# One more weight unit behind the ring's first round, and the norm rows made in expert 3

## The chip, the cores and the metric

The kernel runs on one core of a Trainium2 chip. The core has five engines that run their own instruction lists and wait for each other by semaphores: TensorE (PE, with its weight loads as PEld), VectorE (DVE), ScalarE (ACT), GpSimd (POOL) and SyncE (SP), which here does little but issue transfers. Transfers between HBM and the on-chip memory are carried by 16 DMA engines; SP and ACT each issue into a queue of their own. Time is device time of one execution in microseconds.

## What is computed

One layer of an encoder over 512 tokens of width 1024: three token mixers side by side (neighbourhood attention, grouped-query attention with rotary positions, cross-attention into 256 memory tokens), gated and merged, an output product w_out, a layer norm; then a mixture of 16 experts in which each expert picks its 64 best tokens, and a second layer norm.

```python
branches = jnp.stack([y_na, y_gqa, y_mem], axis=2)
proj = jnp.einsum('bsgk,gkd->bsgd', branches, w_branch[l])
merged = jnp.sum(gates * proj, axis=2)
x = layer_norm(DN_ALPHA * x + merged @ w_out, ln1_g[l], ln1_b[l])
# experts
aff = jax.nn.softmax(x @ w_router, axis=-1)
gate, idx = lax.top_k(jnp.swapaxes(aff, 1, 2), cap)      # 64 tokens each
h = jnp.einsum('becd,edf->becf', x[bidx, idx], w_gate_up)
hg, hu = jnp.split(h, 2, axis=-1)
ye = jnp.einsum('becf,efd->becd', jax.nn.silu(hg) * hu, w_down) * gate[..., None]
x = layer_norm(DN_ALPHA * x + scatter_add(ye, idx), ln2_g[l], ln2_b[l])
```

The experts' weights are float32, 16 x 12 MB, and each is read once.

## The kernel before

The program has no scheduler: every engine carries out its instructions in the order in which the Python code emits them, and a tile framework adds the waits. Tiles with the same tag share memory in turn.

**First half** (mixers, to L1189). PE multiplies weight units of 128 x 1024 that SP streams in (`Stream`, L142 to L192); ACT and DVE split each into a high and a low part (`hi_lo`, L96). Attention runs as a pipeline beside it: `run` (L787) takes one step of attention at the yields of the product generators, and one entry of the background list `bg`, if there is one. For each of the three column groups of grouped-query attention `rope_stages` (L372) gives such entries: s1 square, s2 root mean square, s3 scaling, s4 the rotation in six POOL operations (L402 to L405), then one or two of `sk`/`sq_` (L414, L423), which transpose the result on PE (`heads_T`, L411) and evict it by ACT and DVE. The entries of the last two groups, `a` and `b`, are put in order at L464; among them is `norm_hi`.

**Norm rows.** The gains and shifts of both layer norms are 15 rows of 1024 floats (`lnp`). They are loaded early on SP's queue (`load_norms`, behind the 14th weight unit), cast to a high part on ACT (`norm_hi`, L860) and completed by two DVE operations (`norm_mask`, `norm_lo`), all as background entries, into `gb`, which holds its memory to the end. `ln_row` (L1366) spreads one row over 128 partitions with a PE product; its first user is `residual` in expert 4.

**Second half** (experts, L1568 on). The weights come in units of 128 x 2048 floats (1 MB): `("gu", e, k)`, eight gate/up units of an expert, and `("dn", e, k)`, four down units. `_blocks` (L45) lists the 192 units in the order of their use and deals them, round by round, to the twelve buffers of `RING` (L32), ten of which hold two units. In the first round a block fills its buffer with one load of two units; in the second round (to the 36th unit) and among the last ten each unit is a load of its own. `Ring.load` (L806) issues a block's load on SP's queue; `Ring.upto` fills the first round when the buffers' earlier tenants are done (L977, L1111, L1190); later loads are issued by `Ring.done` (L831) when PE has used the units that the buffer held. SP carries out its loads in order, and with eight completion semaphores in turn it waits for the load eight issues earlier.

Expert e (loop at L1574): the first four (`lead`) gate/up units, with `h_transpose(e - 1)` ahead of the fourth; `down(e - 1)`; for odd e `slots_T(e // 2)`, which turns the one-hot slots of a pair of experts into `GTe` or `GT` (two "homes", used in turn); the other four gate/up units; `act_h(e)`, tanh on ACT and two products on DVE in tiles of the tag "t". After e = 3, 7 and 11 `gather` fetches the next four experts' tokens: 64 products on PE, in chunks of eight through the three "mm" banks, evicted alternately by DVE (L1263) and ACT (L1261). `combine` and `residual` run as side work between units.

The routing's arrays lie in one tile of the tag "bf" (`rt`, L904), among them the affinities `aff` (slot 0).

Of the kernel before, what the change touches and what calls it, by code (L numbers as in the profile page):

```python
# [9 lines left out]
F32 = mybir.dt.float32  # L10
F32R = mybir.dt.float32r
# [3 lines left out]
ALU = mybir.AluOpType  # L15
# [3 lines left out]
P = 128  # L19
D = 1024  # L20
S = 512
KD = 8
NT = 4
NEXP = 16
# [7 lines left out]
RING = (("Q2", 2), ("Q1", 2), ("Q5", 2), ("Q7", 2), ("Q4", 2), ("Q3", 2), ("Q6", 2), ("raw", 1), ("Q9", 2), ("VS", 1),  # L32
        ("G1", 2), ("M", 2))
# [7 lines left out]
def lead(e):  # L41
    return 2 if e == NEXP - 2 else 4


def _blocks():  # L45
    order = []
    for e in range(NEXP - 1):
        order += [("gu", e, k) for k in range(lead(e))]
        if e:
            order += [("dn", e - 1, k) for k in range(4)]  # L50
        order += [("gu", e, k) for k in range(lead(e), KD)]
    order += [("gu", NEXP - 1, k) for k in range(KD)]
    order += [("dn", e, k) for e in (NEXP - 2, NEXP - 1) for k in range(4)]
    blocks, i, r = [], 0, 0
    while i < len(order):
        for tag, n in RING:
            left = ROUNDS.get(tag, len(order)) - r
            if left > 0 and i < len(order):
                keys = order[i:i + n]
                i += n  # L60
                if r and (i < FULL or i > len(order) - N_SINGLE):
                    blocks += [(tag, h, [key]) for h, key in enumerate(keys)]
                else:
                    blocks.append((tag, 0, keys))
        r += 1
    return blocks
# [3 lines left out]
def layer_kernel(ctx: ExitStack, tc: tile.TileContext, xt, xn, first0, wu, bgate, rpb, gains, wrt,  # L70
                 lnp, lnt, wx, csn, nmask, tri, iota, out, dbg=None):
    nc = tc.nc
# [12 lines left out]
    def R(tag, shape, name, dt=F32, bufs=None):  # L85
        return rp.tile(shape, dt, name=name, tag=tag, bufs=bufs)
# [110 lines left out]
    after = {}  # L197
# [61 lines left out]
    nc.sync.dma_start(wr_t, wrt)  # L259
    lnT = cp.tile([P, 5, KD], F32, name="lnT")  # L260
    nc.sync.dma_start(lnT[:, :2], lnt)
    gb = cp.tile([15, D], F32R, name="gb")
    gb_s, gb_c, gb_t = (cp.tile([15, n], F32, name="gb_" + k)[:, :1] for k, n in (("s", 1), ("c", 1), ("t", 33)))
    ident_r = cp.tile([P, P], F32R, name="ident_r")
    gsel = cp.tile([15, 3], F32R, name="gsel")
# [173 lines left out]
    def g_gqa():  # L439
        kk = R("Q6", [P, 4, S], "kk", F32R)  # L440
        qs = R("Q4", [P, 8, S], "qs", F32R)
        ST["b01"] = b01 = R("Q5", [P, 4, 1024], "ropevg")
        b1t = b01[:, 2:4]
        vg = b1t[:, 0, :512].rearrange("p (m f) -> p m f", m=NT)
        ST.update(khh=kk[:, 0:2], klo=kk[:, 2:4], vg=vg, qs=(qs[:, 0:4], qs[:, 4:8]),
                  rope=(vs_t[:, 0], b1t[:, 1]), zr=b01[:, 0:2])
        rope = []
        for q in range(3):
            us = ws.take(2)
            zs = ST["A5" if q % 2 else "A6"][:, 1, :512 if q == 0 else 1024].rearrange("p (m c) -> p m c", m=NT)  # L450
# [12 lines left out]
        a, b = rope[1:]  # L463
        bg.extend([lambda: None, a[4], b[0], a[5], b[1], b[2], b[3], norm_hi, b[4], b[5]])  # L464

    def g_na_v():
        v = ST["b01"][:, 0:2].rearrange("p a (b f) -> p (a b) f", f=S)
# [330 lines left out]
    class Ring:  # L798
# [7 lines left out]
        def load(self):  # L806
            tag, h, keys = self.blocks[self.n]
            n = len(keys)
            src = wx[self.row:self.row + P * n].rearrange("(p j) (h c) -> p (j h) c", j=n, h=2)
            if tag not in self.home:  # L810
                self.home[tag] = R(tag, [P, 2 * dict(RING)[tag], D], f"w{self.n}")
            full = self.home[tag][:, 2 * h:2 * (h + n)]
            nc.sync.dma_start(full, src)
# [38 lines left out]
    norm_raw = []  # L852

    def load_norms():
        norm_raw.append(vs_t[:15, 1])
        nc.sync.dma_start(norm_raw[0], lnp)

    after[14] = [load_norms]

    def norm_hi():  # L860
        nc.scalar.copy(gb, norm_raw[0])

    def norm_mask():
        norm_raw.append(vs_t[:15, 0])
        nc.vector.tensor_scalar(norm_raw[1], gb.bitcast(F32), gb_c, None, op0=ALU.mult)

    def norm_lo():
        nc.vector.scalar_tensor_tensor(gb, norm_raw[0], gb_s, norm_raw[1], op0=ALU.mult, op1=ALU.add)


    run(g_mem())
    dump("mkT", ST["mkT"])
# [6 lines left out]
    yg = R("Q2", [P, 8, S], "yg", F32R)  # L879
    ST["y1"] = (yg[:, 0:4], yg[:, 4:8])  # L880
    at.add([GqaUnit(hp, m) for hp in range(4) for m in range(NT)])
    bg.extend([norm_mask, norm_lo])
    run(g_branch(2, True), 1.0, 3)
    run(g_na_v(), 1.0)
    at.drain()
# [16 lines left out]
    run(g_branch(1, False, between), 0.5)  # L902

    rt = R("bf", [P, 12, 64], "rt")  # L904
    aff = rt[:, 0].rearrange("p (m e) -> p m e", m=NT)
    cnt = rt[:, 2:4].rearrange("p a (m e) -> p m a e", m=NT)
    st_all = rt[:, 5:7].rearrange("p a b -> p (a b)")[:, :96].rearrange("p (m q s) -> p m q s", m=NT, q=4)
    ones_f = rt[:, 7:9].rearrange("p a b -> p (a b)")
# [310 lines left out]
    pos = msk.rearrange("p m a e -> p (m a e)").bitcast(F32).rearrange("p (m e) -> p m e", m=NT)  # L1219
    nc.vector.tensor_tensor(pos, cnt[:, :, 0], cnt[:, :, 1], op=ALU.add)  # L1220
    aff3 = cp.tile([P, NT, NEXP, 3], F16, name="aff3")
    id16 = tri_d
    nc.scalar.copy(id16, ident)
    dump("pos", pos)
# [62 lines left out]
    def gate_up(e, ks):  # L1287
        qd, i = divmod(e, 4)
        if ks[0] == 0:
            GU[e] = (PB("S", f"g{e}"), PB("T", f"u{e}"))  # L1290
        for k in ks:
            w = ring.get("gu", e, k)
            xs = XS[qd][k // 4][:, k % 4, i * CAP:(i + 1) * CAP]
            for b in range(2):
                for hf in range(2):
                    nc.tensor.matmul(GU[e][b][hf * 64:hf * 64 + 64], xs,  # L1296
                                     w[b][:, hf * 512:hf * 512 + 512],
                                     start=(k == 0), stop=(k == KD - 1))
            ring.done("gu", e, k)

# [9 lines left out]
    def h_transpose(e, tp=None):  # L1310
        h = HT[e]
        tp = tp or PB("mm", f"ht{e}", (P, 4, P))
        for c in range(4):
            nc.tensor.transpose(tp[:, c], h[:, c * P:(c + 1) * P], ident)  # L1314
        if e == 0:
            homes.extend((R("tmp", [P, 4, P], "hT", bufs=2), R("tmp", [P, NT, P], "GT", F32R, bufs=2)))
# [30 lines left out]
    def slots_T(pr):  # L1347
        qd, h = divmod(pr, 2)
        gp = PB("mm", f"gT{pr}", (P, NT, P))
        for m in range(NT):  # L1350
            nc.tensor.matmul(gp[:, m], OH[qd][:, m, h * P:(h + 1) * P], id16, start=True, stop=True)
        if pr == 0:
            homes.append(R("bf", [P, NT, P], "GTe", F32R))
        g = homes[1 if pr % 2 else 2]
        GT[pr] = g
        nc.scalar.copy(g, gp)

# [2 lines left out]
    def acc_of(m):  # L1360
# [2 lines left out]
            ACC.update({0: a[:, 0:2], 1: a[:, 2:4]})  # L1363
        return ACC[m // 2][:, m % 2]

    def ln_row(row, h, nm):  # L1366
        bc = PB("mm", nm)
        nc.tensor.matmul(bc, gsel[:, row:row + 1].to_broadcast([15, P]), gb[:, h * 512:h * 512 + 512], start=True, stop=True)
        return bc

    def residual():
# [58 lines left out]
    def last_down(g2, xq, spare):  # L1430
# [116 lines left out]
        scaled_last(3)  # L1547

        def low_rank(m, h):
            nc.tensor.matmul(tl[m, h], rows[:13, m * P:(m + 1) * P], gb[:13, h * 512:h * 512 + 512], start=bool(h), stop=True)  # L1550

        def finish(m, h):
            x = acc_of(m)[:, h * 512:h * 512 + 512]
# [20 lines left out]
    for e in range(NEXP):  # L1574
# [5 lines left out]
        elif e < NEXP - 1:  # L1580
# [8 lines left out]
            for k in range(lead(e)):  # L1589
                if k == lead(e) - 1:  # L1590
                    h_transpose(e - 1)
                gate_up(e, (k,))
                steps(side, side)
                if e == 1:
                    steps(g1)
            if e == 5 or e == 12:
                all_of(side)
            down(e - 1)
            if e % 2:
                slots_T(e // 2)  # L1600
            if e % 4 == 3:
                onehot(e // 4 + 1)
            for k in range(lead(e), KD):
                gate_up(e, (k,))
                if e == NEXP - 2:
                    if k == lead(e):
# [182 lines left out]
```

## Time and profile before

| | us |
|---|---|
| median of 3 runs | 967.41 (966.9 to 967.64) |
| profiled execution, its own time | 966.57 |
| its span, first to last instruction | 964.7 |
| PE busy | 943.4 (98%) |
| DVE busy | 452.3 (47%) |
| ACT busy | 277.0 (29%) |
| POOL busy | 85.5 (9%) |

The clock of PE was 0.997 of full speed over the span. The profile has 40 slices of the span with the busy share of each engine in tenths, the chain of waits that ended last, and groups of instructions by line; the trace behind it gives the instructions in order of time, what ended each idle time, and the transfer rate in any stretch. A row of a timeline reads: start, duration, engine, line, operation, output <- inputs, partitions x elements and type, count, and in brackets the idle time before it with what ended it. A line can be a helper's (L97 and L98 are `hi_lo`). SPq is SP's issue of a transfer: its row shows the issue, not the transfer.

### The profile page before, as it was taken

The numbers are of one execution on the slowest core, as the hardware profiler recorded it, in microseconds if no ns is written. First come the engines' busy times: TensorE is split into PE (matmuls) and PEld (weight loads), VectorE is DVE, ScalarE is ACT, GpSimd is POOL, SyncE is SP. The second block draws the span as 40 slices with busy tenths as digits, with TensorE's granted clock in tenths as the row PEclk, the third lists the DMA queues.
The fourth block names the chain that finished last, engine by engine and source line by source line (L and its number), as shares of the span: only waits on it lengthen the run. The fifth ranks groups of instructions, "written<-read, shape, count | busy, mean of one in ns | idle before, by whom it ended". The sixth has DMA issues, their size and how long they took to land.

```text
span 964.7 us, 13206 instructions
## 1 busy us (share of the span) xinstructions
PE 943.4 (98%) x5406; PEld 615.4 (64%) x5406; DVE 452.3 (47%) x851; ACT 277.0 (29%) x545; POOL 85.5 (9%) x98
## 2 busy tenths in 40 slices
PE   9999999999999999999999999999999999998996
PEld 9899878889888888887885333433344333532344
DVE  6347668774376566237454122653322223231426
ACT  5334454544354454333242111100010000100123
POOL 0102303000032231000023000000000000000003
PEclk9999999999999999999999999999999999999998
DMA  9312221211333322575919999999999999999992
GB/s 361 114 68 66 66 66 44 67 55 57 94 106 111 101 83 73 216 281 205 384 37 387 430 417 432 431 429 431 431 428 432 430 430 431 429 432 430 428 411 95
DMA packets 39193, 251.19 MB, mean 260 GB/s; under 512 B 13007, under 2 KB 13391, under 8 KB 24926
## 3 DMA queue, kind: packets, MB, share of 16 engines
q1 hardware_dynamic: 38414, 249.74, 64.4%
q8 instruction: 42, 0.69, 0.3%
q10 hardware_dynamic: 720, 0.62, 0.2%
q14 instruction: 17, 0.14, 0.0%
HBM read 247.46 MB, written 2.10 MB: 259 GB/s over the span
## 4 chain that ended last, share of the span: by engine, by line
PE 80%; DMA 10%; DVE 6%; ACT 1%; issue 1%; POOL 1%; DVEq 0%; POOLq 0%; ACTq 0%; SPq 0%
DMA w<-in_wx 10%; PE g L1296 10%; PE u L1296 9%; PE y L1331 8%; PE gate L279 4%; PE gate L281 4%; PE gate L280 4%; PE pr L279 2%; PE gy L654 2%; PE ga L1256 2%; PE pr L280 2%; PE pr L281 2%; PE nqk L279 2%; PE nqk L280 2%; PE nqk L281 2%; PE gt L641 1%
## 5 line engine op out<-in xcount | busy, mean ns | idle before, releaser
L1296 PE MATMUL g<-w,xs 128*64 128x512 f32 x512 | 135.0, 606 | 2.6 <-DMA w<-in_wx 2.4
L1296 PE MATMUL u<-w,xs 128*64 128x512 f32 x512 | 131.6, 592 | 0.0
L1331 PE MATMUL y<-w,hT 128*64 128x512 f32 x480 | 106.6, 594 | 3.4 <-DMA w<-in_wx 2.6
L98 DVE TENSOR_TENSOR y<-y,y 64x512 fp32r<-64x512 f32 x30 | 20.7, 689 | 134.5 <-ACT y L97 134.5
L1296 PEld LDWEIGHTS u<-w,xs 128*64 128x64 f32 x512 | 36.8, 137 | 73.1 <-issue 72.3
L97 ACT CAST y<-y 64x512 fp32r<-64x512 f32 x30 | 17.4, 579 | 224.9 <-PE y L1331 213.6
L1331 PEld LDWEIGHTS y<-w,hT 128*64 128x64 f32 x480 | 33.8, 137 | 72.1 <-issue 64.8
L98 DVE TENSOR_TENSOR los<-raw_twin,whi 128x1024 fp32r<-128x1024 f32 x43 | 53.8, 1251 | 52.8 <-ACT whi L97 52.6
L281 PE MATMUL gate<-xh,los 128*128 128x512 f32 x192 | 74.8, 390 | 0.0
L1296 PEld LDWEIGHTS g<-w,xs 128*64 128x64 f32 x512 | 30.7, 136 | 53.7 <-issue 44.8
L279 PE MATMUL gate<-xh,whi 128*128 128x512 f32 x160 | 63.5, 397 | 0.0
L280 PE MATMUL gate<-xl,whi 128*128 128x512 f32 x160 | 62.3, 390 | 0.0
L1403 DVE TENSOR_TENSOR acc<-acc,cb 128x512 f32<-128x512 f32 x56 | 35.6, 683 | 37.8 <-PE cb L1401 37.8
L97 ACT CAST whi<-raw_twin 128x1024 fp32r<-128x1024 f32 x43 | 45.1, 1049 | 8.3 <-PE wo L1094 4.4
L1472 POOL TENSOR_TENSOR acc<-acc,ln2g 128x512 f32<-128x512 f32 x6 | 7.6, 1278 | 429.8 <-DVE l2s L1500 427.8
L98 DVE TENSOR_TENSOR los<-raw_twin,los 128x1024 fp32r<-128x1024 f32 x21 | 26.2, 1247 | 35.0 <-ACT los L97 34.9
L281 PEld LDWEIGHTS gate<-xh,los 128*128 128x128 f32 x192 | 36.0, 188 | 7.7
L630 ACT ACTIVATE att_twin<-gs,nm 128x512 f32<-128x512 f32 x32 | 21.7, 683 | 51.2 <-DVE nm L629 51.2
L1306 ACT ACTIVATE tg<-g 128x512 f32<-128x512 f32 x16 | 9.5, 596 | 88.8 <-PE g L1296 88.8
L279 PEld LDWEIGHTS gate<-xh,whi 128*128 128x128 f32 x160 | 30.0, 188 | 7.1 <-issue 1.2
L280 PEld LDWEIGHTS gate<-xl,whi 128*128 128x128 f32 x160 | 30.1, 188 | 5.9
L1319 DVE COPY hT<-ht 128x512 f32<-128x512 f32 x15 | 10.3, 690 | 44.6 <-PE ht L1314 44.6
(432 smaller groups left out, 1894.8 us busy)
## 6 DMA issues: line engine op xcount, KB each, us to landing
w<-in_wx SPq DMA_DIRECT2D x83, 2048.0 KB
raw_twin<-in_wu SPq DMA_DIRECT2D x65, 512.0 KB
w<-in_wx SPq DMA_DIRECT2D x26, 1024.0 KB
raw<-in_wu SPq DMA_DIRECT2D x8, 512.0 KB
xr<-in_xt SPq DMA_DIRECT2D x4, 512.0 KB
macc<-in_xn SPq DMA_DIRECT2D x2, 1024.0 KB
first<-in_first SPq DMA_DIRECT2D x4, 384.0 KB
bf<-in_rpb SPq DMA_DIRECT2D x64, 24.0 KB
```

The source lines that it names most:

```text
L97: nc.scalar.copy(hi, src)
L98: nc.vector.tensor_tensor(lo, src, hi.bitcast(F32), op=ALU.subtract)
L279: nc.tensor.matmul(acc, w_h, rh[:, k], start=(k == 0), stop=False)
L280: nc.tensor.matmul(acc, w_h, rl[:, k], start=False, stop=False)
L281: nc.tensor.matmul(acc, w_l, rh[:, k], start=False, stop=(k == nk - 1))
L630: nc.scalar.activation(self.p[:, h], self.s[h], AF.Exp, bias=nm[:, h:h + 1], accum_out=self.sm[:, h:h + 1])
L654: nc.tensor.matmul(self.y[h * 64:h * 64 + 64, :P], ST["vg"][:, kc, kvh * 64:kvh * 64 + 64], self.pt[:, h, kc], start=(kc == 0), stop=(kc = ...
L1256: nc.tensor.matmul(g, XH[:, m, c], oh[:, m, sl], start=(m == 0), stop=False)
L1296: nc.tensor.matmul(GU[e][b][hf * 64:hf * 64 + 64], xs, w[b][:, hf * 512:hf * 512 + 512], start=(k == 0), stop=(k == KD - 1))
L1319: nc.vector.tensor_copy(t, tp)
L1331: nc.tensor.matmul(y[o * 64:o * 64 + 64], hT[:, c, hf * 64:hf * 64 + 64], w[j][:, o * 512:(o + 1) * 512], start=(k == 0 and j == 0), stop= ...
L1403: nc.vector.tensor_tensor(a, a, cb, op=ALU.add)
```

## The change

A thirteenth buffer, X, for one unit is put behind the first round: `("gu", 2, 2)`. Its three loads (the up half, and two quarters of the gate half) go into memory of three tags: "gb" (the norm rows'), "tmp" and "bf" (the routing's). It is used once. All later units move to the next place in the ring, so blocks of two now hold units of another pairing, and one load fewer stands at the end.

To make room, `aff` gets memory of its own; the first pair's slots are turned in expert 2 instead of expert 1, when X's "bf" part has been used; the homes are made later; and the norm rows are no longer made in the first half. They are made in expert 3, in two halves of 512 columns, over the memory of X's up half, with loads on ACT's queue and the tag "t" for the scratch. The entry `norm_hi` leaves the background list, and the two at its later end as well.

```diff
     while i < len(order):
+        if r == 1:
+            blocks.append(("X", 0, order[i:i + 1]))
+            i += 1
         for tag, n in RING:
...
-    gb = cp.tile([15, D], F32R, name="gb")
...
-        bg.extend([lambda: None, a[4], b[0], a[5], b[1], b[2], b[3], norm_hi, b[4], b[5]])
+        bg.extend([lambda: None, a[4], b[0], a[5], b[1], b[2], b[3], b[4], b[5]])
...
+            if tag == "X":
+                key, = keys
+                g = [R("bf", [P, 512], "wxa"), R("tmp", [P, 512], "wxb", bufs=2)]
+                u = R("gb", [P, D], "wxc")
+                nc.sync.dma_start(u, src[:, 1])
+                nc.sync.dma_start(g[1], src[:, 0, 512:])
+                nc.sync.dma_start(g[0], src[:, 0, :512])
+                self.t[key] = [g, u]
...
-    after[14] = [load_norms]
-    def norm_hi():
-        nc.scalar.copy(gb, norm_raw[0])
-    def norm_mask():
...
-    def norm_lo():
...
-    bg.extend([norm_mask, norm_lo])
...
-    aff = rt[:, 0].rearrange("p (m e) -> p m e", m=NT)
+    aff = cp.tile([P, NT, NEXP], F32, name="aff")
...
     aff3 = cp.tile([P, NT, NEXP, 3], F16, name="aff3")
+    ring.upto(len(RING) + 1)
...
-                                     w[b][:, hf * 512:hf * 512 + 512],
+                                     w[b][hf] if isinstance(w[b], list) else w[b][:, hf * 512:hf * 512 + 512],
...
-        if pr == 0:
-            homes.append(R("bf", [P, NT, P], "GTe", F32R))
-        g = homes[1 if pr % 2 else 2]
+        if pr < 2:
+            homes.append(R("tmp", [P, NT, P], "GT", F32R, bufs=2) if pr else R("bf", [P, NT, P], "GTe", F32R))
+        g = homes[1 + pr % 2]
...
+    def norm_rows():
+        GB.append(R("gb", [15, D], "gb", F32R))
+        for h in range(2):
+            c = slice(h * 512, h * 512 + 512)
+            raw = R("t", [15, 512], f"nraw{h}", bufs=2)
+            part = R("t", [15, 512], f"npart{h}", bufs=2)
+            nc.scalar.dma_start(raw, lnp[:, c])
+            yield
+            nc.scalar.copy(GB[0][:, c], raw)
+            nc.vector.tensor_scalar(part, GB[0][:, c].bitcast(F32), gb_c, None, op0=ALU.mult)
+            nc.vector.scalar_tensor_tensor(GB[0][:, c], raw, gb_s, part, op0=ALU.mult, op1=ALU.add)
...
                 if k == lead(e) - 1:
                     h_transpose(e - 1)
+                    if e == 3:
+                        nrm = norm_rows()
+                        steps(nrm)
...
-            if e % 2:
-                slots_T(e // 2)
+            if e % 2 and e > 1 or e == 2:
+                slots_T((e - 1) // 2)
             if e % 4 == 3:
                 onehot(e // 4 + 1)
+            if e == 3:
+                steps(nrm)
             for k in range(lead(e), KD):
+                if e == 3 and k == KD - 1:
+                    all_of(nrm)
                 gate_up(e, (k,))
```

`ring.upto(len(RING) + 1)` stands behind the routing's last operation (`pos`), ahead of the first one-hots.

More of the change, by code (lines that the diff above doesn't have):

```diff
@@ L809, in load @@
             src = wx[self.row:self.row + P * n].rearrange("(p j) (h c) -> p (j h) c", j=n, h=2)
+            if tag == "X":
[6 more added lines that the diff above has]
+                self.t[key] = [g, u]
+                self.at[key] = (tag, 0)
+                self.row += P
+                self.n += 1
+                return
             if tag not in self.home:
@@ L850, in layer_kernel @@
     vs_t = R("VS", [P, 2, 1024], "ropesq")
[L852 to L856, printed above, removed]
-    after[14] = [load_norms]
-    def norm_hi():
-        nc.scalar.copy(gb, norm_raw[0])
-    def norm_mask():
-        norm_raw.append(vs_t[:15, 0])
-        nc.vector.tensor_scalar(norm_raw[1], gb.bitcast(F32), gb_c, None, op0=ALU.mult)
-    def norm_lo():
-        nc.vector.scalar_tensor_tensor(gb, norm_raw[0], gb_s, norm_raw[1], op0=ALU.mult, op1=ALU.add)
     run(g_mem())
@@ L1315, in h_transpose @@
         if e == 0:
-            homes.extend((R("tmp", [P, 4, P], "hT", bufs=2), R("tmp", [P, NT, P], "GT", F32R, bufs=2)))
+            homes.append(R("tmp", [P, 4, P], "hT", bufs=2))
         t = R("bf", [P, 4, P], f"hT{e}") if e == NEXP - 1 else homes[0]
@@ L1364, in acc_of @@
         return ACC[m // 2][:, m % 2]
+    GB = []
+    def norm_rows():
[9 more added lines that the diff above has]
+            nc.vector.scalar_tensor_tensor(GB[0][:, c], raw, gb_s, part, op0=ALU.mult, op1=ALU.add)
     def ln_row(row, h, nm):
         bc = PB("mm", nm)
-        nc.tensor.matmul(bc, gsel[:, row:row + 1].to_broadcast([15, P]), gb[:, h * 512:h * 512 + 512], start=True, stop=True)
+        nc.tensor.matmul(bc, gsel[:, row:row + 1].to_broadcast([15, P]), GB[0][:, h * 512:h * 512 + 512], start=True, stop=True)
         return bc
@@ L1549, in low_rank @@
         def low_rank(m, h):
-            nc.tensor.matmul(tl[m, h], rows[:13, m * P:(m + 1) * P], gb[:13, h * 512:h * 512 + 512], start=bool(h), stop=True)
+            nc.tensor.matmul(tl[m, h], rows[:13, m * P:(m + 1) * P], GB[0][:13, h * 512:h * 512 + 512], start=bool(h), stop=True)
         def finish(m, h):
```

## The prediction

> **What bounds the kernel now.** I read the page first, then the windows view over the stretches in which the weights are loaded, then the timelines around every place that the change touches.
>
> ```profile
> span 964.7 us, 13206 instructions
> DMA  9312221211333322575919999999999999999992
> q8 instruction: 42, 0.69, 0.3%
> PE 80%; DMA 10%; DVE 6%; ACT 1%; issue 1%; POOL 1%; DVEq 0%; POOLq 0%; ACTq 0%; SPq 0%
> ```
>
> The DMA digits show two kernels in one. In the first half (digits mostly of 1 to 7) the transfers have time to spare, and the chain of waits runs along PE. From slice 21 on they are at 9, to the end. The windows view puts numbers on the border (columns: stretch, its length, busy time of PE, PEld, DVE, ACT and POOL with instruction counts, PE clock, DMA share, GB/s):
>
> ```profile
> 0.00:20.00 20.00, 18.65 (x140) 18.65 (x141) 12.83 (x21) 12.05 (x13) 0.69 (x6) 1.00 0.92 358
> 483.00:503.00 20.00, 20.00 (x134) 18.09 (x133) 11.38 (x50) 7.21 (x16) 3.65 (x14) 1.00 0.01 1
> 503.00:616.80 113.80, 112.00 (x701) 51.24 (x701) 34.11 (x106) 21.16 (x40) 11.50 (x12) 1.00 0.99 412
> 517.00:520.00 3.00, 2.94 (x24) 1.49 (x24) 1.93 (x9) 0.46 (x1) 0.00 (x0) 1.00 0.88 322
> 522.00:530.00 8.00, 8.00 (x54) 2.94 (x50) 0.41 (x1) 0.91 (x2) 0.00 (x0) 1.00 0.96 355
> 530.00:935.00 405.00, 398.74 (x1988) 152.55 (x1986) 124.58 (x220) 46.13 (x83) 0.00 (x0) 1.00 1.01 429
> ```
>
> For 20 us up to 503 the transfer engines stand still. From 503 they are busy, from 530 to 935 at share 1.01 without a hole, 429 GB/s. A weight unit is 128 x 2048 floats, 1.05 MB, so it takes 1.05/429 = 2.44 us, and nothing that PE does between 530 and 935 can bring the end forward as long as the transfer engines have work. Two things set the end: when the load released at 502.93 goes out, and how many holes the transfers have after it.
>
> ```profile
> 502.93 0.33 SPq L813 DMA_DIRECT2D w<-in_wx  x1
> 515.62 0.33 SPq L813 DMA_DIRECT2D w<-in_wx  x1
> 520.70 0.33 SPq L813 DMA_DIRECT2D w<-in_wx  x1
> 616.80 0.33 SPq L813 DMA_DIRECT2D w<-in_wx  x1
> ```
>
> These are SP's issues of Q9 (which waits for the last product of w_out), of M (the end of the first round), of the second round's first block, and of a block that I need below.
>
> **The added unit.** In the order in which SP is handed its loads, the three loads of X stand directly behind M's. So none of X runs in the idle 20 us: M goes out at 515.62, and X after it, when the engines are already busy. It is in time before the second round's first load (520.70), and its own waits are over by then: the bf part waits for the last reader of the routing's arrays, whose work precedes the first expert's gather. What can X bring? Only holes that it fills: 0.04 x 8 = 0.32 us between 522 and 530. The hole at 517 to 520 (0.12 x 3 = 0.36 us) comes from M's late issue, and X stands behind M. The sum of bytes is the same; a unit loaded earlier is only a unit not loaded later in a queue that is never empty.
>
> Against it: X arrives in rows of 4 and 2 KB instead of 8. The trace has small rows in the first 20 us: 358 GB/s at share 0.92, 389 at full share, and 1.05 MB then takes 2.70 us, 0.26 more than 2.44. The norm rows (15 x 1024 floats, 0.06 MB) move into the full stretch: 0.06/389 = 0.16 us. Sum: -0.32 + 0.26 + 0.16 = +0.1 us. Ends: -0.32 (both extras free) and +0.42 (hole not filled); I take +0.1.
>
> **What leaves the first half.** The norm rows' load and three operations go from there:
>
> ```profile
> 165.19 1.04 ACT L861 CAST gb<-ropesq 15x1024 fp32r<-15x1024 f32 x1
> 186.46 0.73 DVE L865 TENSOR_SCALAR ropesq<-gb,gb_c 15x1024 f32<-15x1024 f32 x1
> 193.18 1.26 DVE L868 SCALAR_TENSOR_TENSOR gb<-ropesq,gb_s 15x1024 fp32r<-15x1024 f32 x1
> ```
>
> PE does not wait for any of them, so their 3.03 us bring nothing. But norm_hi was also a place holder in the background list: one step is taken at each yield, and it stood between b[3] (the rope's six POOL operations, L402 to L405) and b[4] (the four transposes of L411 that read what POOL made). Without it the transposes come one yield earlier. On PE that is from 171.21 to the place where the next gate begins, 162.69. Two rows of the chain of waits (the earlier pass), then the timelines of POOL and PE and the summary of line L405 (count: shortest/median/longest ns):
>
> ```profile
> 118.44 3.92 POOL ropevg L405 x2
> 122.40 0.66 PE rT L411 x4
> ```
>
> ```profile
> 111.51 2.14 POOL L402 TENSOR_TENSOR ropevg<-mkvzs,consts 128x512 f32<-128x512 f32 x1 [20.73 <-DVE mkvzs L392]
> 154.47 1.31 POOL L402 TENSOR_TENSOR ropevg<-mkvzs,consts 128x512 f32<-128x512 f32 x1 [32.13 <-DVE mkvzs L392]
> 159.75 4.16 POOL L405 TENSOR_TENSOR ropevg<-ropevg,ropesq 128x512 f32<-128x512 f32 x2
> 161.67 1.09 PE L654 MATMUL gy<-att_twin,ropevg 128*64 128x128 f32 x16
> 162.69 0.50 PE L279 MATMUL gate<-xh,whi 128*128 128x512 f32 x1
> 171.21 0.66 PE L411 MATMUL rT<-ident,ropevg 128*128 128x128 f32 x4
> L405 POOL TENSOR_TENSOR ropevg<-ropevg,ropesq x4: 1527/2087/2496, 118.4 to 161.4; 128x512 f32<-128x512 f32 x4
> ```
>
> POOL ends at 159.75 + 4.16 = 163.91. In the earlier pass (the chain's rows) PE started 122.40 - 122.36 = 0.04 after POOL's end, having stood waiting for it: the same place, one yield behind b[3]'s twin. So here PE would stand from 162.69 to 163.95: **1.26 us**. The 0.66 us of transposes are moved, not added. Queued behind them on PE are the next gate's 24 matmuls, and behind the same transposes on ACT and DVE the evictions of L431 and L432, all shifted alike. Bounds: with L405 at its fastest (1.53 each) and four multiplications at 1.31, POOL ends at 162.77, 0.12 us of waiting; with the whole pass as long as the first one (111.51 to 122.36, 10.85 us), at 165.32, 2.67 us. I take 1.26, since nothing ahead of it on POOL or DVE changes.
>
> Is it hidden? Between there and the w_out products PE waits for next to nothing:
>
> ```profile
> PE wo L1092 <- DVE tm L955: 0.5, 1, 0.5
> PE x1t L998 <- DVE macc L1015: 0.3, 1, 0.3
> ```
>
> Those are all its waits from 165 to 500, and both are for DVE operations that themselves wait for PE. So the delay reaches the issue at 502.93 whole, and with it everything behind.
>
> **What enters expert three.** norm_rows puts on ACT: issue of half 0's load, cast, issue of half 1's load, cast; on DVE two operations for each half. The order on ACT matters. Half 1's load waits for DVE's second operation of half 0 (it reuses the buffer), the second cast waits for the load, and expert three's tanh (L1306) stands behind that cast. Behind tanh come the gather's evictions, and PE's gather has only three banks.
>
> ```profile
> 602.87 1.42 DVE L1234 TENSOR_TENSOR oh<-iota_t,msk 128x256 f16<-128x256 f32 x4
> 606.80 0.60 ACT L1306 ACTIVATE tg<-g 128x512 f32<-128x512 f32 x1 [3.97 <-PE g L1296]
> 607.43 0.69 DVE L1307 SCALAR_TENSOR_TENSOR tg<-tg,g 128x512 f32<-128x512 f32 x1 [3.15 <-ACT tg L1306]
> 608.24 0.75 DVE L1308 SCALAR_TENSOR_TENSOR h<-tg,gw,u 128x512 f32<-128x512 f32 x1
> 608.90 0.54 DVE L1263 TENSOR_SCALAR xs<-ga,gT,lnT 128x256 f32<-128x256 f32 x1
> 610.18 0.60 PE L1256 MATMUL ga<-oh,xhl 128*128 128x256 f16 x4
> ```
>
> Half 0 is early (its load can go out after expert two's activations). Its DVE operations follow the one-hots (end 604.29) and cost half of the rows above, 0.37 + 0.63 (an estimate, as are the halves below): 605.3, and half 1's load goes out. A small load from issue to use:
>
> ```profile
> 250.21 12.18 SPq L667 DMA_DIRECT2D bf<-in_rpb  x16
> 264.44 6.21 POOL L676 TENSOR_TENSOR bm<-bf,consts 128x256 f32<-128x256 f32 x6 [100.53 <-DMA bf<-in_rpb]
> ```
>
> The last of 16 issues starts near 262.0, its reader at 264.4: 2.4 us. So 607.7; cast 0.52, DVE 1.00: 609.2; tanh 0.60, then 0.69 and 0.75: 611.3, against 608.90 before. The first eviction ends at 611.8, and PE's fourth chunk, which began at 610.18, waits for that bank: PE is **1.6 us** late. The engines are at share 1.01 there, so the load can be slower. Upper bound, behind one whole 2 MB load (4.9 us): PE 6.5 us late.
>
> Does that reach the end? Only if the transfers run dry. By 616.80 the blocks issued since 502.93 hold 46 units, 48.2 MB; moved since 503 are 113.8 x 412 GB/s = 46.9 MB. So 1.3 MB, 3.1 us, lie ahead, less about 1 us until a new load moves: 2.1 us of cover. The change adds a unit (2.44), but the new pairing releases that slot one unit later on PE (1.72, from the rows below): 2.8 us. 1.6 us of lateness fits: nothing. At 6.5 us it would cost 3.7. PE itself makes up the delay: its loads' waits for weights after 520 are 11.3 us.
>
> ```profile
> 616.59 1.03 PE L1296 MATMUL g<-w,xs 128*64 128x512 f32 x4
> 617.45 1.03 PE L1296 MATMUL u<-w,xs 128*64 128x512 f32 x4
> ```
>
> ```profile
> PEld g L1296 <- DMA w<-in_wx: 5.7, 5, 2.1
> PEld y L1331 <- DMA w<-in_wx: 5.6, 4, 2.1
> ```
>
> A unit on PE is two such groups of four: each row shows 1.03 for four overlapping ones, and the next starts 0.86 later, so 1.72. The norm rows' first reader, L1368 in expert four, stands behind the late tanh in any case.
>
> The Trainium skill, page "DMA: Bandwidth & Descriptors", section "Queues, rings and completion order", speaks against this step: an engine alternates between queues only at packet borders and drains a whole packet of some 9 to 17 descriptors first. By that rule the late bound would be the likelier; no row of this trace shows a small load beside a full queue.
>
> slots_T(0) moves from expert one to two: the same four matmuls and one ACT copy, no cost. aff in memory of its own changes no order.
>
> **Sum.** +1.26 (PE waits for POOL) + 0.1 (transfers) + 0 (expert three) = +1.4 us on the profiled execution, span 964.7, its own time 966.57: 967.9. The median shown is 967.41, 0.84 above it: **968.8 us**.
>
> **Rivals.**
> 1. The transfers run dry: half 1's load waits behind a whole weight load, the gather stands, the slot at 616.80 goes out late. It decides from 2.8 us of lateness on. For it: the full queue. Against it: 42 instruction loads on a queue of their own (q8) go through beside the weights, and the waits of PE name none. At the bound +3.7: 972.5.
> 2. POOL is in time and the sum is nothing: the fast bound, 0.12 + 0.1: 967.6. Against it the first pass, which did stall PE.
> 3. The other side, faster: X does what a deeper ring should. If the three loads escape M's wait, or the holes in the averages hide more than I see, a whole unit drops out of the saturated stretch: -2.44, and with the POOL wait at 0.12, 965.1; in full, 966.2. Against it: X's place behind M, and share 1.01.
>
> **How the numbers follow.** Forecast 0.58, rival 1 0.18, rival 2 0.13, rival 3 0.11. About 0.2% (1.9 us) is what a measurement of this kernel can tell from no change. The forecast's own range, 967.2 to 970.5 (the POOL bounds and the transfers' ends), crosses the upper limit of 969.3: 0.13 of its 0.58 is slower. Slower: 0.13 + 0.18 = 0.31. Faster: 0.07 of rival 3. The rest, 0.62, is the same. The range 966.6 to 971.0 takes in the forecast, rival 2 and the smaller forms of 1.
>
> **What would show it.** Right: a wait of rT (L413 in the new numbering) for POOL of 1.2 us near 163; the issue after w_out later by as much; DMA share 1.0 between 522 and 530; the second gather's evictions some 2 us later behind expert three's matmuls. Wrong: no such wait; a share under 1 between 616 and 635; loads of X before the routing ends.

## The result, and the profile after

The changed kernel took 974.54 us in the median of 6 runs (971.98 to 974.85), the kernel before 967.52 beside it (6 runs, 966.9 to 969.02): ratio 1.0072, 95% interval 1.0061 to 1.0082. It is slower by 7.0 us. The profiled execution was the shortest of the six, 971.98 with a span of 970.2, and stands 5.4 us above the one before (966.57) by its own time, 5.5 by its span. The forecast was 968.8, its range up to 971.0.

From the page of the kernel after: the span, the transfers' digits, and the shares of the chain of waits.

```profile
span 970.2 us, 13228 instructions
DMA  9311111111332322575819999999999999999992
PE 79%; DVE 7%; DMA 7%; ACT 2%; POOL 2%; issue 2%; ACTq 0%; POOLq 0%; DVEq 0%; SPq 0%
```

By these lines it is the same kernel: a first half on PE's path, a second one in which the transfers are full. Only the stretches show where they are not. First the kernel before, then the kernel after (stretch, length, busy time of PE, PEld, DVE, ACT and POOL, PE clock, DMA share, GB/s).

```profile
590.00:600.00 10.00, 10.00 (x50) 3.27 (x46) 0.69 (x1) 0.00 (x0) 0.00 (x0) 1.00 1.01 431
600.00:616.00 16.00, 16.00 (x116) 9.45 (x116) 7.22 (x19) 4.60 (x8) 0.00 (x0) 1.00 1.00 428
616.00:620.00 4.00, 4.00 (x20) 1.24 (x18) 3.78 (x6) 0.00 (x0) 0.00 (x0) 1.00 1.02 438
620.00:640.00 20.00, 19.25 (x90) 6.30 (x88) 13.51 (x15) 1.75 (x3) 0.00 (x0) 1.00 1.01 431
```

```profile
522.00:530.00 8.00, 8.00 (x54) 3.14 (x54) 0.82 (x2) 0.92 (x2) 0.00 (x0) 1.00 0.98 367
530.00:580.00 50.00, 50.00 (x292) 18.32 (x290) 9.81 (x26) 5.62 (x12) 0.00 (x0) 1.00 1.01 429
590.00:600.00 10.00, 10.00 (x50) 3.41 (x48) 0.69 (x1) 0.00 (x0) 0.00 (x0) 1.00 1.01 377
600.00:616.00 16.00, 12.24 (x74) 5.72 (x71) 6.60 (x13) 4.02 (x8) 0.00 (x0) 1.00 1.00 394
616.00:620.00 4.00, 3.48 (x20) 2.54 (x20) 1.35 (x3) 0.64 (x2) 0.00 (x0) 0.58 1.02 438
620.00:640.00 20.00, 19.24 (x102) 7.24 (x100) 12.42 (x20) 2.04 (x4) 0.00 (x0) 1.00 0.93 364
640.00:900.00 260.00, 257.27 (x1244) 99.36 (x1245) 79.43 (x137) 26.36 (x47) 0.00 (x0) 1.00 1.01 430
```

Read the last column as bytes. From 590 to 640 the kernel before moves 10 x 431 + 16 x 428 + 4 x 438 + 20 x 431 = 21.5 MB, the kernel after 19.1 MB by the same sum. The missing 2.42 MB are 5.6 us at 430 GB/s, and the span is longer by 5.5. From 503 to 590 both moved the same, 407 GB/s, although the transfers began 0.85 us later in the kernel after; behind 640 the rates agree again. So the whole loss of this execution lies in 50 us, in two forms: a lower rate at full share (590 to 616), and a share of 0.93 (620 to 640), where the transfers ran dry. In the same stretch PE stood 3.8 us (12.24 of 16), and its clock fell to 0.58.

What held PE is on ACT. Its timeline in the kernel after (start, duration, operation, in brackets the idle time before it and what ended it):

```profile
603.59 0.61 ACT L1372 CAST gb<-nraw 15x512 fp32r<-15x512 f32 x1
606.39 0.33 ACTq L1370 DMA_DIRECT2D nraw<-in_lnp  x1
611.71 0.62 ACT L1372 CAST gb<-nraw 15x512 fp32r<-15x512 f32 x1 [7.51 <-DMA nraw<-in_lnp]
613.73 0.60 ACT L1302 ACTIVATE tg<-g 128x512 f32<-128x512 f32 x1 [1.40 <-DVE gb L1374]
614.22 0.56 ACT L1257 ACTIVATE xs<-ga,lnT,gT 128x256 f32<-128x256 f32 x1
```

Half 1's load goes out at 606.39, its cast starts at 611.71: 5.3 us from issue to use. Tanh stands behind the cast and behind half 1's second DVE operation, whose buffer it takes over (the 1.40 in its brackets): 613.73 instead of 606.80. PE's gather (L1252, L1254) waits for the banks that only the evictions behind tanh clear; the first row is that of the kernel before, where the gather has ended:

```profile
614.82 1.08 PE L1296 MATMUL g<-w,xs 128*64 128x512 f32 x4
```

```profile
610.60 0.60 PE L1254 MATMUL ga<-oh,xhl 128*128 128x256 f16 x4
614.83 0.60 PE L1252 MATMUL ga<-oh,xhl 128*128 128x256 f16 x4 [3.63 <-ACT xs L1257]
615.26 0.60 PE L1254 MATMUL ga<-oh,xhl 128*128 128x256 f16 x4
616.52 1.01 PE L1252 MATMUL ga<-oh,xhl 128*128 128x256 f16 x4 [0.65 <-ACT xs L1257]
617.33 1.06 PE L1254 MATMUL ga<-oh,xhl 128*128 128x256 f16 x4
...
621.65 1.08 PE L1292 MATMUL g<-w,xs 128*64 128x512 f32 x4
```

Two waits, 3.63 and 0.65. The two groups of four right behind the first still take 0.60 us, the next ones about 1.0. The first unit of expert four starts at 621.65. SP's issues:

```profile
503.78 0.33 SPq L827 DMA_DIRECT2D w<-in_wx  x1
516.50 0.33 SPq L827 DMA_DIRECT2D w<-in_wx  x1
625.35 0.33 SPq L827 DMA_DIRECT2D w<-in_wx  x1
```

The slot that went out at 616.80 before is due one unit later now, 618.52, and went out at 625.35, 6.8 us late. Of these, 0.85 come from the first half, and 6.0 from expert three. And far ahead of all this, PE's waits in the kernel after (total, times, longest) and the place itself:

```profile
PE ga L1252 <- ACT xs L1257: 4.3, 2, 3.6
PE rT L413 <- POOL ropevg L407: 3.0, 2, 1.8
```

```profile
159.31 4.14 POOL L407 TENSOR_TENSOR ropevg<-ropevg,ropesq 128x512 f32<-128x512 f32 x2
163.51 0.66 PE L413 MATMUL rT<-ident,ropevg 128*128 128x128 f32 x4 [1.18 <-POOL ropevg L407]
```

### The profile page after: what moved, and what is told of

Same layout as the page of the kernel before. It is cut to its first block, busy times and chain, and to the rows that moved or that the text cites. A ratio compares the mean times of both kernels' runs of the same rounds, so it can differ in the third digit from the quotient of the medians.

```text
span 970.2 us, 13228 instructions
## 1 busy us (share of the span) xinstructions
PE 944.8 (97%) x5406; PEld 615.6 (63%) x5406; DVE 453.6 (47%) x853; ACT 277.3 (29%) x546; POOL 85.1 (9%) x98
## 4 chain that ended last, share of the span: by engine, by line
PE 79%; DVE 7%; DMA 7%; ACT 2%; POOL 2%; issue 2%; ACTq 0%; POOLq 0%; DVEq 0%; SPq 0%
PE g L1292 10%; PE y L1327 9%; PE u L1292 9%; DMA w<-in_wx 6%; PE gate L281 4%; PE gate L283 4%; PE gate L282 4%; PE ga L1252 2%; PE cb L1410 2%; PE pr L281 2%; PE nqk L281 1%; PE nqk L282 1%; PE nqk L283 1%; PE pr L282 1%; PE pr L283 1%
```

## The experiments

Ratios are to the kernel before, run beside each; the intervals are 95%.

**The place in the list.** The kernel after, with

```diff
-        bg.extend([lambda: None, a[4], b[0], a[5], b[1], b[2], b[3], b[4], b[5]])
+        bg.extend([lambda: None, a[4], b[0], a[5], b[1], b[2], b[3], lambda: None, b[4], b[5]])
```

> The kernel after, with an empty step put back in the background list where the norm rows' copy stood; nothing else changes. Theory (step A): PE's wait of 1.46 us for POOL at 163.5 goes, PE is by about 1.2 us earlier at the issue behind w_out (503.78 in the profile after), and the time falls from 974.5 by 1.2 us, to about 973.3. Rival: the order of the list does not matter to the end because PE has spare time later; then the time stays at 974.5.

Ratio 1.0060 (1.0043 to 1.0076), 971.88 us. PE's wait and the issue behind w_out in this run:

```profile
PE rT L413 <- POOL ropevg L407: 1.8, 1, 1.8
```

```profile
502.42 0.33 SPq L827 DMA_DIRECT2D w<-in_wx  x1
```

The second wait (1.2 us) is gone, and the issue is 1.36 us earlier than at 503.78 (in another pair below, with the rows spread, it is 1.15). The ratio is 0.0012 lower, 1.2 us, which is within the intervals; the same edit shows the same 0.0012 once more below, again within them. Step A holds for PE's wait and for the issue. That it reaches the end whole is likely, but not shown.

**Norm rows spread over two experts.** The kernel after, with half 0 in expert two, half 1 in expert three, each load issued at the transposes and finished at the last unit.

```diff
             nc.vector.scalar_tensor_tensor(GB[0][:, c], raw, gb_s, part, op0=ALU.mult, op1=ALU.add)
+            yield
...
-                    if e == 3:
+                    if e == 2:
                         nrm = norm_rows()
+                    if e in (2, 3):
                         steps(nrm)
...
-            if e == 3:
-                steps(nrm)
...
-                if e == 3 and k == KD - 1:
-                    all_of(nrm)
+                if e in (2, 3) and k == KD - 1:
+                    steps(nrm)
```

> The kernel after, with the norm rows' first half loaded and worked out in expert two and the second in expert three, each load issued at the transposes of the expert before and read only at the expert's last chunk, over 10 us later. Theory 1 (half 1's load was late): ACT no longer stands, the gather's gap of 3.9 us and the clock of 0.58 at 616 to 620 go, the share between 620 and 640 is 1.0 again, and the time falls by about 5 us, to 969.5. Theory 2 (X, with its short rows and the spread of landings that follows it, slows the transfers): the time stays within 1 us of 974.5 and the GB/s of 600 to 640 stay below 400.

Ratio 1.0026 (1.0014 to 1.0037): 0.0046, 4.4 us of the 7.0, are gone, with X still there. Theory 2 falls.

**The norm rows alone.** The kernel before, with `norm_rows` in expert three as in the kernel after (into `gb`, which keeps its own memory), an empty step in the list, and no X.

```diff
-    after[14] = [load_norms]
...
-    bg.extend([norm_mask, norm_lo])
...
+                    if e == 3:
+                        nrm = norm_rows()
+                        steps(nrm)
...
+            if e == 3:
+                steps(nrm)
...
+                if e == 3 and k == KD - 1:
+                    all_of(nrm)
```

> The kernel before, with one part of the change alone: the norm rows made in expert three as the changed kernel does, an empty step in the background list, no X. Theory 1: this part carries nearly all of the loss: half 1's load takes 5 us or more from issue to landing, the second gather is about 6 us late, the transfers run dry behind it, and the time is 971.5 to 973 (against 967.5). Theory 2: without X the transfers keep their pace; the time is 967.5 to 968.5.

Ratio 1.0071 (1.0056 to 1.0086), 973.46 us: this part alone loses as much as the whole change, rather more than theory 1 expected. Its stretches:

```profile
600.00:616.00 16.00, 12.05 (x70) 5.94 (x69) 7.00 (x14) 3.93 (x7) 0.00 (x0) 0.93 1.01 425
616.00:620.00 4.00, 3.35 (x17) 2.15 (x16) 0.94 (x2) 0.57 (x1) 0.00 (x0) 0.50 0.98 422
620.00:640.00 20.00, 19.25 (x103) 7.62 (x103) 12.11 (x20) 1.71 (x3) 0.00 (x0) 0.98 0.75 287
```

```profile
624.47 0.33 SPq L813 DMA_DIRECT2D w<-in_wx  x1
```

There is no slower stretch ahead of the gather here (425 up to 616), but a deeper hole behind it: 0.75. The slot of 616.80 goes out at 624.47, 7.7 us late, and the span is 7.0 longer (971.7). So the slower transfers of the kernel after seem to add nothing of their own in its profile. A likely reason, which no run isolates: bytes that move more slowly before the slot opens are still there when the queue would run empty.

**X alone.** The kernel after with both edits (empty step, rows spread).

> The kernel after with both edits of the two runs above (empty step, norm rows spread over two experts), so that of the change X alone is left. Theory 1: 968.0 to 968.5, what X costs by itself, close to the kernel before (967.5). Theory 2: the time is still 972 or more.

Ratio 1.0014 (1.0002 to 1.0026), 967.64 us; the span, 964.8, is that of the kernel before (964.7). What is left of the change costs 1.4 us by the ratio, with an interval from 0.2 to 2.5, and nothing in the profile. The profile speaks for one execution only: of the ten, six lie between 965.98 and 968.06, the traced one (966.62) among them, and four between 969.78 and 970.74. Beside the run with the rows spread, the empty step is again worth 0.0012.

**Half 1's load alone.** The kernel after; both halves are loaded into the two buffers of "t" at the transposes, the rest stays in its places. The first factor is applied in place, so that no scratch is needed.

```diff
+        for h in range(2):
+            nc.scalar.dma_start(raws[h], lnp[:, h * 512:h * 512 + 512])
         for h in range(2):
...
-            nc.scalar.dma_start(raw, lnp[:, c])
             yield
-            nc.scalar.copy(GB[0][:, c], raw)
-            nc.vector.tensor_scalar(part, GB[0][:, c].bitcast(F32), gb_c, None, op0=ALU.mult)
-            nc.vector.scalar_tensor_tensor(GB[0][:, c], raw, gb_s, part, op0=ALU.mult, op1=ALU.add)
+            nc.scalar.copy(GB[0][:, c], raws[h])
+            nc.vector.tensor_scalar(raws[h], raws[h], gb_s, None, op0=ALU.mult)
+            nc.vector.scalar_tensor_tensor(GB[0][:, c], GB[0][:, c].bitcast(F32), gb_c, raws[h], op0=ALU.mult, op1=ALU.add)
```

> The kernel after, with both halves of the norm rows loaded at the transposes of expert two (half 1 no longer waits for half 0's second operation); the cast and the two operations of each half stay where they are in expert three, with the factors applied in another order so that no other buffer is needed. Theory (half 1's late load is the whole cause, not the work that the norm rows put on ACT and DVE): tanh and the gather stand as in the run with the rows spread over two experts, 4.5 us under the kernel after, about 969.7. Rival (the norm rows' work on ACT and DVE in expert three is itself part of it): 971 or more.

Ratio 1.0013 (1.0004 to 1.0023), 968.32 us. The ACT timeline and the stretches of this run:

```profile
603.62 1.13 ACT L1372 CAST gb<-nraw 15x512 fp32r<-15x512 f32 x2
607.68 0.60 ACT L1302 ACTIVATE tg<-g 128x512 f32<-128x512 f32 x1 [2.94 <-PE g L1292]
610.45 0.56 ACT L1257 ACTIVATE xs<-ga,lnT,gT 128x256 f32<-128x256 f32 x1 [2.17 <-PE ga L1254]
```

```profile
616.00:620.00 4.00, 4.00 (x20) 1.23 (x18) 3.71 (x11) 0.19 (x1) 0.00 (x0) 1.00 1.00 430
620.00:640.00 20.00, 19.24 (x88) 6.31 (x90) 13.63 (x14) 1.76 (x3) 0.00 (x0) 1.00 1.01 430
```

```profile
619.39 5.29 SPq L827 DMA_DIRECT2D w<-in_wx  x2
```

Now tanh and the evictions wait for PE, not PE for them, the slot goes out at 619.39 (the first issue of the row), 6.0 us earlier than at 625.35, and there is no hole. All the work of the norm rows is still in expert three; only half 1's load is earlier. It was worth 0.0059, 5.7 us (4.4 by the run with the rows spread, which also removes the late load).

**The clock.** The kernel after, with multiplications that nobody reads in PE's wait.

```diff
         for f in range(KD):
+            if qd == 1 and f == 3:
+                keep_warm(32)
             g = PB("mm", f"ga{qd}{f}")[:, :n * CAP]
```

> The kernel after, with 32 multiplications of the identity, read by nobody, between the second gather's third and fourth chunk, where PE waits 3.6 us; nothing else changes. Theory: of the gather's lateness of 6 us, 1.7 to 3.4 us are the halved clock behind the wait, not the wait; with PE busy the clock stays at 1.00 between 614 and 620, the chunks take 0.60 instead of 1.06 us, the slot is released 1.7 us earlier or more, and the time falls by 1.7 to 3 us. Rival: the clock drop hides behind the evictions, whose pace sets the gather; then the time stays at 974.5.

Ratio 1.0074 (1.0061 to 1.0088). The filler was twice too long, as PE's timeline shows, so this run decides nothing about the clock:

```profile
611.03 7.31 PE L1140 MATMUL warm<-ident 128*128 128x128 f32 x64
618.17 0.60 PE L1254 MATMUL ga<-oh,xhl 128*128 128x256 f16 x4
```

With half of it:

> The kernel after with 16 multiplications of the identity in the same place as in the run with 32. There each was carried out as two instructions (64 of 0.115 us, 7.31 us), so that it outlasted the wait it was to fill; 16 make 3.7 us, as long as the wait. Theory: the clock stays at 1.00 behind the wait, the gather ends 1.7 us earlier than in the profile after (621.65) or more, the slot is released by as much earlier, and the time falls by 1.7 to 3 us, to a ratio of 1.004 to 1.0055. Rival: the clock falls all the same, or the evictions set the pace; ratio 1.007 as the kernel after.

Ratio 1.0049 (1.0033 to 1.0064), 971.4 us. PE's timeline:

```profile
610.95 3.74 PE L1140 MATMUL warm<-ident 128*128 128x128 f32 x32
615.04 0.60 PE L1254 MATMUL ga<-oh,xhl 128*128 128x256 f16 x4 [0.36 <-ACT xs L1259]
...
616.62 0.60 PE L1254 MATMUL ga<-oh,xhl 128*128 128x256 f16 x4 [0.54 <-DVE xs L1261]
```

The groups keep 0.60, the waits for ACT and DVE stay, and the slot goes out at 624.08, 1.3 us earlier than at 625.35. By the ratios the fall of the clock was worth 0.0023, some 2.2 us of the 7.0; from the two intervals the difference can be estimated only to between 0.4 and 4 us. (The profiled execution of this kernel, 981.37, was the longest of its five, for the reason under the last heading; the other four lie between 971.08 and 972.68.)

**PE late by itself.** The kernel before, nothing of the change in it, with `keep_warm(26)` in the same place.

> The kernel before, nothing of the change in it, with 26 multiplications of the identity (52 instructions, 6.0 us) between the second gather's third and fourth chunk: PE is late by as much as in the kernel after, with no small load, no wait of ACT and no fall of the clock. Theory (the loss is PE's lateness less the cover of 2.1 us that this kernel has): the slot of 616.80 is released at 622.8, the transfers run dry for about 3.9 us, and the time is 3.9 us above before, ratio 1.004. Rival (PE's lateness is absorbed later, and what costs in the kernel after is the small loads among the weights): within 1 us of before.

Ratio 1.0051 (1.0037 to 1.0064), 971.64 us, span 969.8:

```profile
609.91 5.97 PE L1145 MATMUL warm<-ident 128*128 128x128 f32 x52
622.34 0.33 SPq L813 DMA_DIRECT2D w<-in_wx  x1
```

```profile
616.00:620.00 4.00, 4.00 (x39) 3.58 (x38) 1.09 (x2) 1.13 (x2) 0.00 (x0) 1.00 0.89 381
620.00:640.00 20.00, 19.25 (x95) 6.48 (x94) 13.03 (x21) 1.72 (x3) 0.00 (x0) 1.00 0.82 329
```

With no small load and no fall of the clock, PE late by 5.5 us (622.34 against 616.80) makes the same hole and a span 5.1 us longer. The mechanism behind the gather needs nothing but the lateness. But only 0.4 us of it were covered, not 2.1.

**X's up half ahead of Q9.** The run with both edits, and a load that does not wait for w_out:

```diff
+        def x_early(self):
+            row = P * sum(len(k) for _, _, k in self.blocks[:len(RING)])
+            src = wx[row:row + P].rearrange("(p j) (h c) -> p (j h) c", j=1, h=2)
+            self.x_up = R("gb", [P, D], "wxc")
+            nc.sync.dma_start(self.x_up, src[:, 1])
...
     ring.upto(8)
+    ring.x_early()
```

> The kernel of the run with both edits (empty step, norm rows spread over two experts), and X's up half, whose memory is free from the start, loaded ahead of Q9, where SP waits for w_out and the transfers stand still. Theory (what bounds after 530 is the number of bytes that are left, so only bytes moved before 503 help): 0.52 MB leave the full stretch, 0.52/430 = 1.2 us, so 1.2 us under the run with both edits, which stood 0.9 over the kernel before: about 966.5 beside a before of 966.8, the same or slightly faster. Rival: what X costs is its form (narrow rows, the spread of landings), not its place; then it stays at 0.9 over the kernel before.

Ratio 1.0006 (0.9995 to 1.0017), against 1.0014 (1.0002 to 1.0026): in the direction expected, inside the intervals, so not settled.

**A version from the three edits** (empty step, both loads early, X's up half early).

> The kernel after with the empty step, both halves of the norm rows loaded at the transposes of expert two, and X's up half loaded ahead of Q9. Theory: the three edits add up: 1.0013 (both loads early) less 1.2 us (step A) less 0.8 us (early half) gives 0.9993, some 0.7 us under the kernel before. Rival: the early half brings nothing; 1.000.

Ratio 0.9994 (0.9985 to 1.0003), 966.19 us (11 runs, 965.28 to 967.86). It is clearly faster than the kernel after; against the kernel before the interval includes no change.

## Why the prediction was wrong

**Step A, PE waits for POOL: right for the wait.** 1.26 us were forecast; the second wait measures 1.2. The issue behind w_out is 0.85 later than in the kernel before, and 1.15 and 1.36 later than in the two runs that differ by the empty step alone. The ratio shows 1.2 twice, each time within its intervals, so that it reached the end whole, as argued, is likely but not shown.

**The added unit: right in its place, its effect open.** X went out behind M (516.50). The share of 522 to 530 rose from 0.96 to 0.98 in the kernel after, and not to 1.0. By bytes X seems to fill more than the 0.32 us of the forecast. In the run with X alone and in PE late by itself, which has no X, the load behind w_out goes out at the same time (502.62 and 502.66); from 503 to 590 they moved 413 and 408 GB/s, 0.4 MB more with X, or 1.0 us of transfers. Yet no gain came through to the end. With half 1's load early, 1.3 us of the loss stay (1.0013, 0.4 to 2.2 us); if 1.2 of them are step A, 0.1 is left for X, as forecast, but the run with X alone says 1.4 (0.2 to 2.5). Whether X in the end gains or costs a little can't be told from these runs, and that the forecast of +0.1 fits one of them is no proof of its terms.

**"What enters expert three": the step that failed.** The order of events was forecast as it came: half 1's load out behind half 0's DVE operations (605.3 forecast; 606.39 less the 0.85 by which this part of the kernel runs late is 605.5), the cast behind it, tanh, the evictions, the gather. The mis-sized term is the load, and with it PE's lateness: 1.6 us were forecast, 6.0 came (621.65, against 614.82 before and 0.85 of earlier delay). The load was put at 2.4 us, from a load in the first half, where the transfers have time to spare; the trace shows 5.3, beside a full queue. PE's fourth chunk starts 3.8 us late instead of 1.6 (614.83 less 0.85, against 610.18). The second wait (0.65) and about 1.4 us of slow multiplications, the next term, make up the rest.

The prediction named an upper bound, behind a whole weight load, 6.5 us of lateness for PE, and took the lower one. The bound came closer to the 6.0, but in part by luck: it holds 4.9 us more for the load, where 2.9 came, and nothing for the second wait and the clock. The row for the price came from a stretch whose transfer engines were mostly idle. The Trainium skill, page "DMA: Bandwidth & Descriptors", section "Queues, rings and completion order", had pointed there, as the prediction itself noted: an engine drains a whole packet of some 9 to 17 descriptors before it turns to another queue. An estimate by it, with one descriptor for each 16 KB row of a two-unit load: at 430/16 GB/s for one engine a row takes 0.61 us, nine of them 5.5 us. The 5.3 of the trace is near that in size, but the trace does not show the rule at work: by its packet records half 1's first row moves 3.4 us after the issue, and all 15 rows within the next 0.8 us. Each of the 20 such loads in the ten profiles that have them starts its first row 3.3 to 4.1 us after its issue; for the load of 502.93, issued to idle engines, this is 0.95. Why the queue adds about 2.4 us and not more is open.

**A term that was missing: the clock.** No step had it. The trace's clock record has PE at half its clock for 3.41 us from 615.94; the four groups from 616.52 to 619.63 take 3.1 us, where four at 0.44 from start to start take 1.75. That is 1.4 us, and the filled wait brings the slot 1.3 us earlier. In the norm rows alone the half clock lasts 6.83 us (0.93, 0.50 and 0.98 in the three stretches). The granted clock of the profiled execution was 0.995, that of the other five 0.993, as in the norm rows alone: another 3.41 us at half the clock would make this difference (0.5 x 3.41 of 970 is 0.0018). So they probably had the longer fall, and this is likely why the profiled execution was the shortest of its six, but their clock over time is not on record. The Trainium skill, page "TensorE: Matmul & The Clock Gate", section "Part 1: The HAM clock gate", says that an idle window of about 3.4 us puts the clock to half; the trace agrees: 3.63 us of idle time, then the granted clock of 0.58 between 616 and 620.

**The cover: too large.** 2.1 us before and 2.8 after were worked out from bytes in flight, less 1 us until a new load moves. The lateness of the slot less the growth of the span gives 0.4 (5.5 less 5.1, PE late by itself), 0.7 (7.7 less 7.0, the norm rows alone) and 1.3 (6.8 less 5.5, the kernel after). The extra unit's 0.7 fits these figures; the base is smaller by 1.4 to 1.7. Here the queue did not hold its rate until its last byte: the 0.89 of 616 to 620 comes before the late issue of 622.34. Nor did the next load start at full rate. The packet records of PE late by itself show 16 transfers at a time at 619.0, 10 at 619.5, 2 at 621.0 and none at 622.5; behind the issue of 622.34 there are 7 at 623.5, 14 at 624.5, and 16 only at 625.5. The forecast had 1 us for the start, and full rate before and behind it.

**Rival 1 is what happened**, at 972.5 with a chance of 0.18. Its mechanism, its place and the slot that it named are those of the trace. Its figure is partly luck: for the profiled execution it comes to 971.6, against 971.98, because a load that was too long makes up for a cover that was too large, and for the second wait and the clock, which it lacks. It is 2 us short of the median, which lies 2.6 above the profiled execution here and 0.84 there. Its "against" (instruction loads pass beside the weights) was no evidence: the row gave their number and share, not how long one took.

The parts in the runs: some 1.2 us for the place in the list, 4.4 to 5.7 for half 1's late load (with the clock in it), of 7.0 together. They do not simply add up: the norm rows alone lose 6.9 without X and without step A, in a trace whose slot is 7.7 us late and whose half clock is twice as long. One late load of 30 KB stopped ACT, ACT stopped PE, PE held a slot of 2 MB, and the transfers, which bound the second half, ran dry.

## What to carry to other kernels

Price a load by a row from a stretch in which its queue's neighbours are as busy as where it is to run; where there is none, do not make the idle row the forecast: the 5.3 us here lie between the idle row's 2.4 and the 7.3 of the bound, and above the middle. Issue a small load one stage before its reader, with a buffer that is free then: here the same work in the same places cost 5.7 us less. And before an instruction that waits for a transfer is put on an engine, look for what stands behind it in that engine's order, up to the engine that releases the next large load.

An entry in a list that interleaves engines can be a delay that a kernel needs, even an empty one: what is removed is not only its work.

## What was not expected of the hardware

In the kernel after, the transfers were slower at full share between 590 and 616 (377 and 394 GB/s at 1.01 and 1.00). The profiled execution of the kernel with 16 multiplications shows the same for much longer, and then the usual rate:

```profile
590.00:702.00 112.00, 110.34 (x548) 45.48 (x544) 47.44 (x74) 11.48 (x20) 0.00 (x0) 1.00 1.01 379
702.00:900.00 198.00, 188.86 (x937) 73.24 (x938) 52.25 (x98) 20.42 (x36) 0.00 (x0) 1.00 1.01 429
```

112 us at 379 instead of 429 are 13 us of transfers, and that execution was about 10 us longer than its neighbours. Such a stretch shows in the profiles of five of the nine kernels that have X and make the norm rows among the experts: 377, 352, 398, 388 and 382 GB/s between 590 and 600 (the kernel after, the empty step, 32 and 16 multiplications, the version from three edits). A sixth, the one with X's up half ahead of Q9, has a short one earlier (381 and 383 GB/s from 570 to 580), as its half 0 is loaded earlier (566.24). It is not there in the kernel before (431), in PE late by itself (441) and in the norm rows without X (430), nor in the two other runs with the rows spread. It begins some 3 to 4 us behind the issue of half 0's load, at full share and with PE's clock at 1.00. What makes it was not tried and stays open. It may also be what spreads the executions of the runs with X (966.0 to 970.7 for X alone, 968.0 to 971.7 with the rows spread, against 965.9 to 968.8 for the kernel before beside them), but only one execution of each was traced. In the kernel after it seems to cost nothing beyond the hole, since the norm rows alone lose as much without it; where it lasts as long as in the execution with 16 multiplications, it costs more than all the rest.
